# Conditioning in blocks of 1024 columns, four K tiles per visit and two wide groups in a hybrid retention and mLSTM step

## The chip, the cores and the metric

The kernel runs on one core of one Trainium2 chip. The metric is the device time of a run in microseconds. Before the change the median of three runs is 2097.72 us (2091.96 to 2099.7).

The core has several engines with their own instruction queues: TensorE (PE in the profile; PEld is its weight load), VectorE (DVE), ScalarE (ACT), GpSimd (POOL) and SyncE (SP), from whose queue most loads are issued. Some DMAs are issued from GpSimd's queue, in order with its arithmetic.

## The reference

One layer is computed for 128 context tokens (the prompt) and 256 latent tokens (the sample), of width 2048. A conditioning vector for each of the two kinds of tokens is multiplied with `w_mod` to six parts of 2048 numbers: shift, scale and gate of the mixer (parts 0, 1, 2) and of the channel mixer (parts 3, 4, 5).

```
mod_ctx = silu(c_ctx) @ w_mod + b_mod          # w_mod is 2048 x 12288
mod_lat = silu(c) @ w_mod + b_mod
sh1, sc1, g1, sh2, sc2, g2 = split(mod, 6)
h = ln(x) * (1 + sc1) + sh1
mix = mixer(h)                                 # h @ w_in, 8 heads, then @ w_out
x = ln(ALPHA * x + g1 * mix) * ln1_g + ln1_b
h = ln(x) * (1 + sc2) + sh2
x = ln(ALPHA * x + g2 * ffn(h)) * ln2_g + ln2_b
```

The mixer has four retention heads and four mLSTM heads of 256 columns, run forwards and backwards; `ffn` is a gated convolution with 5504 inner columns. All is fp32. The outputs are both kinds of tokens and the final states of the prompt.

## The kernel before

There are 384 tokens, three tiles of 128 (`NT`), and 2048 features, 16 K tiles of 128 (`KT`). Weights and activations are split into a rounded high part and a rest (`split`, L116: a ScalarE cast gives `hi`, a subtraction gives `lo`), and each product is three matmuls: high by high, high by rest, rest by high (`mm_a`, L179, and `mm_b`, L186). The rest of a weight block is made on VectorE, and every so-manieth on GpSimd: every sixth in stage one and in the mixer, none in the output projection, every second in the first part of the channel mixer (`share_splits`, L127).

The program is written against tiles and buffers; a planner works out the waits and the order of each engine's queue, from the order of the program and from its own estimates of the times. A buffer of a pool with `bufs=1` is written again only when its last reader is done, and a DMA that waits for that holds up what stands behind it in its queue.

**Conditioning.** It is computed in two ways, piece by piece between other work. A `Stepper` (L297) holds a generator and, at each step of the main work, lets it go on by so many pieces (its rate).

- `mod_tensor` (L246) computes by features on TensorE: for each K tile one product with the two conditioning vectors, padded to 32 columns (`ct`), into one of four column groups of a PSUM bank (`g = kt % 4`, 32 partitions each), so that the groups hold partial sums. ScalarE copies the bank (`mr`), small products add up the groups and turn the row into columns (`modf`), and VectorE adds the bias. One visit takes `nk` K tiles. It serves parts 0 and 1 in stage one and half of part 4 in the output projection.
- `mod_vector` (L270) computes by rows on VectorE: blocks of 512 columns, for each K tile and each of the two vectors one multiply-add over 512 columns (L287, L284 for the first) into `acc` (`macc`). At the end of a block two products with ones, into column groups 0 and 1, sum over the partitions (L292), VectorE adds the bias (L293), and two stores from GpSimd's queue write the rows into DRAM (`modrow`, L295). The block's bias `bt` is loaded from GpSimd's queue (L276); `acc` and `bt` have one buffer each. It serves parts 2 and 3 and the other half of part 4 (`NV = 2` blocks) in the mixer and part 5 in the channel mixer. `vec_raws` loads two K tiles by 512 columns at a time (512 KB, L234), from SP's queue, where the weights (L141) are loaded too.

**Stage one** (L373 to L471) normalises the tokens and then goes through the K tiles in groups (`groups`): for each group `hs` modulates and splits its K tiles, and `units` multiplies them with the weights of two retention heads; the partial sums go from PSUM into SBUF, added by VectorE from the second group on (`spill`, L388). While a group is multiplied, the conditioning of the next one runs in the `Stepper` at 1.2 pieces per unit, of which there are six a group. The groups are 1, 1, 2, 2, 2, 2, 2, 2 and 2 K tiles, nine in all; a visit's load is always 1 MB, so it has 16, or 8, K tiles of one or two columns' tiles.

**Mixer** (L473 to L866). First come constants and gates (`log_sigmoid`, L508), rotary embedding and the attention of the first two heads; then six more heads, each projected (`proj_a`, `proj_b`) while the attention of the one two places earlier runs. After each weight block comes a step of `mods2` (L614) at rate 0.9. `gnr` and `gnm` (L482 to L485) are rows of the heads' norms, loaded at the beginning and read by `head_tail` (L663 or L665).

**Output projection** (L911 to L959): four blocks of 512 columns by 16 K tiles, two K tiles to a weight block. In the second and third block a step of `mods4` (L927), rate 1.5, follows each weight block; it visits two K tiles of 512 columns at a time (`nk = 2`), with five buffers of 512 KB loaded four ahead. `mod_from_rows` fetches the rows of parts 3 and 4 that the mixer stored.

**Channel mixer** (L1051 on): the up projections with `mods5` (L1120, part 5, rate 0.85) in the first twelve tiles, then the down projections and the last norm.

Of the kernel before, what the change touches and what calls it, by code (L numbers as in the profile page):

```python
# [9 lines left out]
F32 = mybir.dt.float32  # L10
# [5 lines left out]
P = 128  # L16
D = 2048
# [65 lines left out]
def hybrid_step(ctx, tc, ca, cb, x_prompt, x_sample, state_ret, state_c, state_n, state_m, c, c_ctx,  # L83
# [143 lines left out]
    def mod_loads(newraw, pieces, lag):  # L227
        """The pieces' loads in turn, each lag pieces ahead of its use."""
# [11 lines left out]
    NV = 2  # L240

    def vec_raws(mp, blocks):
        return mod_loads(lambda: mp.tile([P, 1024], F32, tag="mraw", name="mraw"),
                         [(q, 2, part * D + j * 512, 512) for part, j in blocks for q in range(0, KT, 2)], 2)

    def mod_tensor(part, k0, n, psp, sbp, raws, nk):  # L246
        """Blocks of the conditioning by features: products on the tensor engine."""
# [22 lines left out]
    def mod_vector(part, psp, mp, raws, js=range(4)):  # L270
        """A part of the conditioning by rows: products on the vector engine, into DRAM."""
        for j in js:
            col = part * D + j * 512
            acc = mp.tile([P, 2, 512], F32, tag="macc", name="macc", bufs=1)
            bt = mp.tile([64, 512], F32, tag="mbt", name="mbt", bufs=1)
            nc.gpsimd.dma_start(out=bt, in_=b_mod[:, col:col + 512].to_broadcast([64, 512]))  # L276
            for q in range(8):
                raw = next(raws)
                for kk in range(2):
                    kt = 2 * q + kk  # L280
                    for v in range(2):
                        src = raw[:, kk * 512:(kk + 1) * 512]
                        if kt == 0:
                            nc.vector.tensor_scalar(out=acc[:, v, :], in0=src, scalar1=ct[:, kt, v:v + 1],  # L284
                                                    scalar2=None, op0=ALU.mult)
                        else:
                            nc.vector.scalar_tensor_tensor(out=acc[:, v, :], in0=src, scalar=ct[:, kt, v:v + 1],  # L287
                                                           in1=acc[:, v, :], op0=ALU.mult, op1=ALU.add)
                yield
            ps = psp.tile([64, 512], F32, tag="ps", name="modr")  # L290
            for v in range(2):
                nc.tensor.matmul(ps[32 * v:32 * v + 32, :], lhsT=ones, rhs=acc[:, v, :], start=True, stop=True)  # L292
            nc.vector.tensor_tensor(bt, ps, bt, op=ALU.add)  # L293
            for v in range(2):
                nc.gpsimd.dma_start(out=modrow[part, v:v + 1, j * 512:(j + 1) * 512], in_=bt[32 * v:32 * v + 1, :])  # L295
# [77 lines left out]
    groups = [(0, 1), (1, 1)] + [(k, 2) for k in range(2, KT, 2)]  # L373
# [39 lines left out]
    with ExitStack() as p0:  # L413
# [51 lines left out]
        for g in range(len(groups)):  # L465
            nxt = Stepper(mods(g + 1) if g + 1 < len(groups) else iter(()), 1.2)
# [7 lines left out]
    with p1:  # L474
# [4 lines left out]
        with tc.issue_after(on_pool[0]):  # L479
            cs = tab.tile([P, C_B], F32, name="cs")  # L480
            nc.gpsimd.dma_start(out=cs, in_=cb)
            gnr = tab.tile([P, 1024], F32, name="gnr")  # L482
            rows_bcast(gnr, gn_ret.rearrange("a h v -> a (h v)"), 1024)
            gnm = tab.tile([P, 1024], F32, name="gnm")
            rows_bcast(gnm, gn_mlstm.rearrange("a h v -> a (h v)"), 1024)  # L485
# [22 lines left out]
        def log_sigmoid(dst, x, shape, tg):  # L508
            def tmp(n):
                return gp.tile(shape, F32, tag=f"ls{tg}{n}", name=f"ls{tg}{n}")  # L510
            e, u, dd, ln = tmp(0), tmp(1), tmp(2), tmp(3)
# [3 lines left out]
            nc.vector.tensor_scalar(out=dd, in0=u, scalar1=-1.0, scalar2=None, op0=ALU.add)  # L515
            nc.vector.tensor_tensor(dd, e, dd, op=ALU.subtract)
            nc.scalar.activation(ln, u, AF.Ln)
            nc.vector.reciprocal(u, u)
            nc.vector.tensor_tensor(dd, dd, u, op=ALU.mult)
            nc.vector.tensor_tensor(ln, ln, dd, op=ALU.add)  # L520
            nc.vector.scalar_tensor_tensor(out=dst, in0=x, scalar=0.0, in1=ln, op0=ALU.min, op1=ALU.subtract)

        log_sigmoid(lgb, lgb, [P, 8], "t")
# [21 lines left out]
        # gates  # L545
# [67 lines left out]
        raws2 = vec_raws(mp, [(part, j) for part in (2, 3) for j in range(4)] + [(4, j) for j in range(NV)])  # L613
# [81 lines left out]
        def mlstm_attn(h, q, k, vx, og):  # L695
# [65 lines left out]
            finish = head_tail(hh, og, gnm, h, 8 + 2 * h, h == NH - 1)  # L761
# [86 lines left out]
        deferred = []  # L848
        for pf, af, h in heads:
            fn, ph, got = pend.pop(0)  # L850
            deferred.append(fn(ph, *got))
            pend.append((af, h, pf(h)))
        mods2.finish()
# [57 lines left out]
    with ExitStack() as p2:  # L911
# [5 lines left out]
        for kt in range(KT - 2, KT):  # L917
# [18 lines left out]
        def w_out_block(nb, ks):  # L936
            ps = [(pat if nb == 1 else pmm).tile([P, 512], F32, tag="ps", name="pso") for _ in range(NT)]
            for k0 in range(0, ks, 2):
# [12 lines left out]
                if nb == 2 and k0 == 8:  # L951
                    mod_from_rows(4, 4 * NV, pat, sb2, "sc2", 1.0)
# [252 lines left out]
```

## Time and profile before

| what | value |
|---|---|
| median of three runs | 2097.72 us |
| range of the runs | 2091.96 to 2099.7 us |
| profiled execution, first to last instruction (its span) | 2095.7 us |
| mean granted TensorE clock | 0.983 |
| DMA traffic | 352.34 MB, mean 168 GB/s |
| `raw<-in_w_in` loads of 256 KB / 512 KB | 152 / 48 |
| `mraw<-in_w_mod` loads of 512 KB | 128 |
| `wm<-in_w_mod` loads of 1 MB | 32 |

For the profiled execution no other time is given than its span; it lies within the range of the timed runs. The profile's page gives busy times of the engines, the span in 40 slices, the chain of work that ended last, and the costliest groups of instructions by line, with their count, busy time, mean duration and what ended the idle time ahead of them. The other views used here are busy time by stretches of the span (its columns are the stretch, its length, then busy time and count for PE, PEld, DVE, ACT and POOL, the granted clock, the DMA share and GB/s), the timeline of one engine (start, duration, engine, line, operation, output and inputs, count, and in square brackets the idle time before it and what ended it), the waits summed by who waited for whom (total, times, longest), and the instructions of one tile (least, median and greatest duration in ns, first and last start). The stages lie in the span as follows: stage one up to about 230 us, the mixer to about 820, the output projection to about 910, the norms after it to about 990, the channel mixer to the end.

### The profile page before, as it was taken

What the parts mean: (1) busy time and instruction counts of PE and PEld (TensorE: products, weight loads), DVE (VectorE), ACT (ScalarE), POOL (GpSimd) and SP (SyncE); (2) the same over time, 40 slices, a digit from 0 to 9 for tenths busy, and PEclk for the clock granted to TensorE, in tenths of its full rate; (3) what the DMA queues carried; (4) which work ended last, traced back from release to release, by engine and by line L of the source; (5) the groups of instructions that cost most, each with busy time, mean ns of one, the idle gap of its engine ahead of it and who ended that gap; (6) DMA issues with size and microseconds to landing.
All of it is one profiled execution on the core that took longest, in us unless ns stands there. A gap on an engine that the chain in (4) does not pass through costs nothing.

```text
span 2095.7 us, 27032 instructions
## 1 busy us (share of the span) xinstructions
PE 2016.2 (96%) x10361; PEld 1758.6 (84%) x10361; DVE 1308.6 (62%) x2095; ACT 683.3 (33%) x1053; POOL 316.6 (15%) x246
## 2 busy tenths in 40 slices
PE   6999899999999998998999999999999999999996
PEld 4777678798888876676998988999989998999985
DVE  4666879888798765367787744444344444444458
ACT  4223333233344443126322322333222332233331
POOL 1111333232122211014234300000000000000004
PEclk9999999999999999998999999999999999999998
DMA  9975777777796535733656644444334443434441
GB/s 330 349 238 189 115 169 214 211 206 232 194 210 191 153 120 189 276 117 102 194 183 202 220 137 130 122 121 130 121 129 123 122 130 121 129 113 131 145 148 70
DMA packets 283296, 352.34 MB, mean 168 GB/s; under 512 B 16271, under 2 KB 213200, under 8 KB 282016
## 3 DMA queue, kind: packets, MB, share of 16 engines
q1 hardware_dynamic: 278896, 340.09, 54.2%
q0 software_dynamic: 4272, 10.54, 1.5%
q8 instruction: 81, 1.33, 0.3%
q14 instruction: 47, 0.39, 0.1%
HBM read 343.16 MB, written 7.41 MB: 167 GB/s over the span
## 4 chain that ended last, share of the span: by engine, by line
PE 81%; DVE 8%; DMA 4%; issue 2%; POOL 2%; SPq 1%; ACT 1%; POOLq 0%; DVEq 0%; ACTq 0%
PE psu L184 11%; PE psu L182 11%; PE psu L183 11%; PE psd L192 5%; PE psd L190 5%; PE psd L191 5%; PE psb L190 3%; PE psb L191 3%; PE psa L182 3%; PE psb L192 3%; DVE macc L287 3%; PE psa L184 3%; PE psa L183 3%; PE modps L255 2%; PE pso L190 2%
## 5 line engine op out<-in xcount | busy, mean ns | idle before, releaser
L118 DVE TENSOR_TENSOR lo<-raw,hi 128x1024 fp32r<-128x1024 f32 (+3 forms) x437 | 454.4, 1048 | 504.3 <-ACT hi L117 504.0
L117 ACT CAST hi<-raw 128x1024 fp32r<-128x1024 f32 (+3 forms) x487 | 436.5, 908 | 952.6 <-PE psu L183 350.8
L184 PE MATMUL psu<-ah,lo 128*128 128x384 f32 x1376 | 467.3, 340 | 9.4 <-DVE lo L118 4.8
L183 PE MATMUL psu<-al,hi 128*128 128x384 f32 x1376 | 467.7, 340 | 0.0
L182 PE MATMUL psu<-ah,hi 128*128 128x384 f32 x1376 | 467.1, 341 | 0.0
L287 DVE SCALAR_TENSOR_TENSOR macc<-mraw,ct,macc 128x512 f32<-128x512 f32 x420 | 348.9, 878 | 28.7 <-DMA mraw<-in_w_mod 28.7
L184 PEld LDWEIGHTS psu<-ah,lo 128*128 128x128 f32 x1376 | 259.5, 189 | 10.0 <-DVE lo L118 5.1
L182 PEld LDWEIGHTS psu<-ah,hi 128*128 128x128 f32 x1376 | 259.5, 189 | 3.5 <-ACT y L1084 0.8
L183 PEld LDWEIGHTS psu<-al,hi 128*128 128x128 f32 x1376 | 259.5, 189 | 0.1
L118 POOL TENSOR_TENSOR lo<-raw,hi 128x1024 fp32r<-128x1024 f32 (+1 forms) x50 | 154.4, 3091 | 392.5 <-ACT hi L117 358.5
L192 PE MATMUL psd<-hi,fal 128*128 128x512 f32 (+1 forms) x484 | 191.3, 395 | 0.0
L191 PE MATMUL psd<-lo,fah 128*128 128x512 f32 (+1 forms) x484 | 189.5, 392 | 0.0
L190 PE MATMUL psd<-hi,fah 128*128 128x512 f32 (+1 forms) x484 | 188.1, 393 | 0.0
L182 PE MATMUL psa<-ah,hi 128*128 128x384 f32 x512 | 180.1, 355 | 1.7 <-DVE og L392 1.7
L184 PE MATMUL psa<-ah,lo 128*128 128x384 f32 x512 | 176.5, 347 | 5.1 <-POOL lo L118 3.6
L183 PE MATMUL psa<-al,hi 128*128 128x384 f32 x512 | 178.1, 348 | 0.0
L200 POOL TENSOR_TENSOR brs<-veps,mhalf 128x1 f32<-128x1 f32 x12 | 13.4, 1116 | 994.0 <-DVE veps L198 993.9
L191 PE MATMUL psb<-lo,ah 128*128 128x512 f32 x384 | 154.1, 401 | 3.3 <-POOL lo L118 2.5
L192 PE MATMUL psb<-hi,al 128*128 128x512 f32 x384 | 153.2, 399 | 0.0
L190 PE MATMUL psb<-hi,ah 128*128 128x512 f32 x384 | 151.2, 405 | 0.3 <-ACT hi L117 0.3
L182 PEld LDWEIGHTS psa<-ah,hi 128*128 128x128 f32 x512 | 98.0, 192 | 19.0 <-issue 11.3
L191 PEld LDWEIGHTS psd<-lo,fah 128*128 128x128 f32 x484 | 90.8, 188 | 22.5
(300 smaller groups left out, 2408.9 us busy)
## 6 DMA issues: line engine op xcount, KB each, us to landing
raw<-in_w_up SPq DMA_DIRECT2D x168, 512.0 KB, 3.7
mraw<-in_w_mod SPq DMA_DIRECT2D x128, 512.0 KB, 5.4
raw<-in_w_down SPq DMA_DIRECT2D x84, 512.0 KB, 3.6
raw<-in_w_in SPq DMA_DIRECT2D x152, 256.0 KB, 5.1
wm<-in_w_mod SPq DMA_DIRECT2D x32, 1024.0 KB, 7.9
raw<-in_w_in SPq DMA_DIRECT2D x48, 512.0 KB, 6.9
raw<-in_w_out SPq DMA_DIRECT2D x32, 512.0 KB, 4.2
out<-r SPq DMA_DIRECT2D x12, 256.0 KB, 2.0
```

Source lines behind the costliest of these rows:

```text
L117: nc.scalar.copy(dst_hi, src)
L118: mark["lo"] = (eng or nc.vector).tensor_tensor(out=dst_lo, in0=src, in1=dst_hi.bitcast(F32), op=ALU.subtract).ins
L182: nc.tensor.matmul(ps, lhsT=hi[:, s], rhs=ah, start=start, stop=False)
L183: nc.tensor.matmul(ps, lhsT=hi[:, s], rhs=al, start=False, stop=False)
L184: nc.tensor.matmul(ps, lhsT=lo[:, s], rhs=ah, start=False, stop=stop)
L190: nc.tensor.matmul(ps, lhsT=ah[:, t], rhs=hi[:, s], start=start, stop=False)
L191: nc.tensor.matmul(ps, lhsT=ah[:, t], rhs=lo[:, s], start=False, stop=False)
L192: nc.tensor.matmul(ps, lhsT=al[:, t], rhs=hi[:, s], start=False, stop=stop)
L200: mark["pow"] = nc.gpsimd.tensor_tensor(out=out, in0=v[:, :n], in1=mhalf[:, :n], op=ALU.pow).ins
L255: nc.tensor.matmul(ps[32 * g:32 * g + 32, :w], lhsT=ct[:, kt, :], rhs=raw[:, kk * w:(kk + 1) * w], start=kt < 4, stop=kt >= 12)
L287: nc.vector.scalar_tensor_tensor(out=acc[:, v, :], in0=src, scalar=ct[:, kt, v:v + 1], in1=acc[:, v, :], op0=ALU.mult, op1=ALU.add)
```

## The change

- `mod_vector` works in blocks of 1024 columns: `acc` is 128 x 2 x 1024, a load is one K tile by 1024 columns, a multiply-add covers 1024 columns, and the block's sums are four products into all four column groups, followed by one addition over 128 partitions and four stores; the bias comes in two loads. `NV` is 1 block, which is the same half of part 4.
- `mods4` takes four K tiles per visit: loads of 1 MB in three buffers, two ahead, at rate 0.9.
- The last eight K tiles of stage one form two groups of four in place of four groups of two; ahead of a group of four the conditioning runs at 2.0 pieces per unit. Its visits then have four K tiles of 512 columns, and the weight blocks of `q` and `k` four K tiles.
- `gnm` shares one buffer with `gnr` and is loaded once the first mLSTM head is at the front of the pending heads. `log_sigmoid` works with two temporaries fewer and one VectorE instruction fewer.

```diff
-    NV = 2
+    NV = 1
...
-                         [(q, 2, part * D + j * 512, 512) for part, j in blocks for q in range(0, KT, 2)], 2)
+                         [(kt, 1, part * D + j * 1024, 1024) for part, j in blocks for kt in range(KT)], 2)
...
+    def mod_vector(part, psp, mp, raws, js=range(2)):
...
+            col = part * D + j * 1024
+            acc = mp.tile([P, 2, 1024], F32, tag="macc", name="macc", bufs=1)
+            bt = mp.tile([P, 512], F32, tag="mbt", name="mbt", bufs=1)
+            for hf in range(2):
+                nc.gpsimd.dma_start(out=bt[64 * hf:64 * hf + 64, :],
+                                    in_=b_mod[:, col + hf * 512:col + (hf + 1) * 512].to_broadcast([64, 512]))
+            for kt in range(KT):
                 raw = next(raws)
+                for v in range(2):
+                    if kt == 0:
+                        nc.vector.tensor_scalar(out=acc[:, v, :], in0=raw, scalar1=ct[:, kt, v:v + 1],
+                                                scalar2=None, op0=ALU.mult)
+                    else:
+                        nc.vector.scalar_tensor_tensor(out=acc[:, v, :], in0=raw, scalar=ct[:, kt, v:v + 1],
+                                                       in1=acc[:, v, :], op0=ALU.mult, op1=ALU.add)
                 yield
+            ps = psp.tile([P, 512], F32, tag="ps", name="modr")
+            for hf in range(2):
+                for v in range(2):
+                    g = 2 * hf + v
+                    nc.tensor.matmul(ps[32 * g:32 * g + 32, :], lhsT=ones, rhs=acc[:, v, hf * 512:(hf + 1) * 512],
+                                     start=True, stop=True)
             nc.vector.tensor_tensor(bt, ps, bt, op=ALU.add)
+            for hf in range(2):
+                for v in range(2):
+                    g = 2 * hf + v
+                    nc.gpsimd.dma_start(out=modrow[part, v:v + 1, j * 1024 + hf * 512:j * 1024 + (hf + 1) * 512],
+                                        in_=bt[32 * g:32 * g + 1, :])
...
-    groups = [(0, 1), (1, 1)] + [(k, 2) for k in range(2, KT, 2)]
+    groups = [(0, 1), (1, 1), (2, 2), (4, 2), (6, 2), (8, 4), (12, 4)]
...
-            nxt = Stepper(mods(g + 1) if g + 1 < len(groups) else iter(()), 1.2)
+            wide = g + 1 < len(groups) and groups[g + 1][1] == 4
+            nxt = Stepper(mods(g + 1) if g + 1 < len(groups) else iter(()), 2.0 if wide else 1.2)
...
-            nc.vector.tensor_scalar(out=dd, in0=u, scalar1=-1.0, scalar2=None, op0=ALU.add)
-            nc.vector.tensor_tensor(dd, e, dd, op=ALU.subtract)
+            nc.vector.scalar_tensor_tensor(out=e, in0=u, scalar=-1.0, in1=e, op0=ALU.add, op1=ALU.subtract)
...
+            if pend[0][0] is mlstm_attn and not gn_m:
+                gn_m.append(tab.tile([P, 1024], F32, tag="gn", name="gnm"))
+                rows_bcast(gn_m[0], gn_mlstm.rearrange("a h v -> a (h v)"), 1024)
...
-        mp = pool("mp2", 5, p2m, reuse_waits="tile")
-        raws4 = mod_loads(lambda: mp.tile([P, 1024], F32, tag="mraw", name="mraw"),
-                          [(q, 2, 4 * D + j * 512, 512) for j in range(NV, 4) for q in range(0, KT, 2)], 4)
-        mods4 = Stepper(chain(*[mod_tensor(4, 4 * j, 4, pmm, sb2, raws4, 2) for j in range(NV, 4)]), 1.5)
+        mp = pool("mp2", 3, p2m, reuse_waits="tile")
+        raws4 = mod_loads(lambda: mp.tile([P, 2048], F32, tag="mraw", name="mraw"),
+                          [(q, 4, 4 * D + j * 512, 512) for j in range(2 * NV, 4) for q in range(0, KT, 4)], 2)
+        mods4 = Stepper(chain(*[mod_tensor(4, 4 * j, 4, pmm, sb2, raws4, 4) for j in range(2 * NV, 4)]), 0.9)
```

More of the change, by code (lines that the diff above doesn't have):

```diff
@@ L268, in mod_tensor @@
         yield
-    def mod_vector(part, psp, mp, raws, js=range(4)):
+    def mod_vector(part, psp, mp, raws, js=range(2)):
         for j in js:
[L273 to L277, printed above, removed]
-                raw = next(raws)
[L279 to L288, printed above, removed]
-                yield
[L290 to L295, printed above, removed]
@@ L481, in hybrid_step @@
             nc.gpsimd.dma_start(out=cs, in_=cb)
-            gnr = tab.tile([P, 1024], F32, name="gnr")
+            gnr = tab.tile([P, 1024], F32, tag="gn", name="gnr")
             rows_bcast(gnr, gn_ret.rearrange("a h v -> a (h v)"), 1024)
-            gnm = tab.tile([P, 1024], F32, name="gnm")
-            rows_bcast(gnm, gn_mlstm.rearrange("a h v -> a (h v)"), 1024)
             m0b = tab.tile([P, 8], F32, name="m0b")
@@ L510, in tmp @@
                 return gp.tile(shape, F32, tag=f"ls{tg}{n}", name=f"ls{tg}{n}")
-            e, u, dd, ln = tmp(0), tmp(1), tmp(2), tmp(3)
+            e, u, ln = tmp(0), tmp(1), dst
             nc.scalar.activation(e, x, AF.Abs)
@@ L514, in log_sigmoid @@
             nc.vector.tensor_scalar(out=u, in0=e, scalar1=1.0, scalar2=None, op0=ALU.add)
-            nc.vector.tensor_scalar(out=dd, in0=u, scalar1=-1.0, scalar2=None, op0=ALU.add)
-            nc.vector.tensor_tensor(dd, e, dd, op=ALU.subtract)
+            nc.vector.scalar_tensor_tensor(out=e, in0=u, scalar=-1.0, in1=e, op0=ALU.add, op1=ALU.subtract)
             nc.scalar.activation(ln, u, AF.Ln)
             nc.vector.reciprocal(u, u)
-            nc.vector.tensor_tensor(dd, dd, u, op=ALU.mult)
-            nc.vector.tensor_tensor(ln, ln, dd, op=ALU.add)
+            nc.vector.tensor_tensor(e, e, u, op=ALU.mult)
+            nc.vector.tensor_tensor(ln, ln, e, op=ALU.subtract)
             nc.vector.scalar_tensor_tensor(out=dst, in0=x, scalar=0.0, in1=ln, op0=ALU.min, op1=ALU.subtract)
-        log_sigmoid(lgb, lgb, [P, 8], "t")
+        lth = lgb
+        lgb = tab.tile([P, 8], F32, name="lgb2")
+        log_sigmoid(lgb, lth, [P, 8], "t")
         def rope(dst, a, b, sb):
@@ L610, in hybrid_step @@
         sb = pool("sb1", 2, p1, reuse_waits="tile")
-        raws2 = vec_raws(mp, [(part, j) for part in (2, 3) for j in range(4)] + [(4, j) for j in range(NV)])
+        raws2 = vec_raws(mp, [(part, j) for part in (2, 3) for j in range(2)] + [(4, j) for j in range(NV)])
         mods2 = Stepper(chain(mod_vector(2, pat, mp, raws2), mod_vector(3, pat, mp, raws2),
@@ L760, in mlstm_attn @@
                                                        in1=hh[:, tt, :], op0=ALU.mult, op1=ALU.add)
-            finish = head_tail(hh, og, gnm, h, 8 + 2 * h, h == NH - 1)
+            finish = head_tail(hh, og, gn_m[0], h, 8 + 2 * h, h == NH - 1)
             for d in range(2):
@@ L847, in hybrid_step @@
         pend = [(ret_attn, h, first[h]) for h in range(2)]
-        deferred = []
+        deferred, gn_m = [], []
         for pf, af, h in heads:
@@ L951, in w_out_block @@
                 if nb == 2 and k0 == 8:
-                    mod_from_rows(4, 4 * NV, pat, sb2, "sc2", 1.0)
+                    mod_from_rows(4, 8 * NV, pat, sb2, "sc2", 1.0)
             return ps
@@ L1119, in hybrid_step @@
     mp3 = pool("mp3", 3, p3m, reuse_waits="tile")
-    mods5 = Stepper(mod_vector(5, pps, mp3, vec_raws(mp3, [(5, j) for j in range(4)])), 0.85)
+    mods5 = Stepper(mod_vector(5, pps, mp3, vec_raws(mp3, [(5, j) for j in range(2)])), 0.85)
     a += ups(2, 10)
```

## Prediction

> **What bounds the kernel now.** I read the page first, then busy time by stage, because its shares are averages over stages with different limits.
>
> ```profile
> span 2095.7 us, 27032 instructions
> PE 2016.2 (96%) x10361; PEld 1758.6 (84%) x10361; DVE 1308.6 (62%) x2095; ACT 683.3 (33%) x1053; POOL 316.6 (15%) x246
> ```
>
> ```profile
> 0.00:220.00 220.00, 200.27 (x1345) 150.49 (x1346) 139.66 (x338) 71.52 (x169) 28.16 (x29) 1.00 0.83 268
> 300.00:820.00 520.00, 506.07 (x2401) 429.82 (x2400) 418.21 (x719) 196.65 (x337) 133.36 (x114) 0.99 0.65 184
> 820.00:910.00 90.00, 90.00 (x376) 59.30 (x376) 36.85 (x44) 22.78 (x23) 1.12 (x2) 0.98 0.81 281
> 1200.00:2050.00 850.00, 850.00 (x4367) 786.57 (x4366) 381.74 (x493) 259.08 (x305) 0.00 (x0) 1.00 0.42 129
> ```
>
> The columns are the stretch, its length, busy time of PE, PEld, DVE, ACT and POOL, granted clock, DMA share and GB/s. TensorE is the bound: full in the output projection (820 to 910), 506 of 520 us in the mixer, full in the untouched last 850 us. VectorE, at 418 of 520 us in the mixer, has slack there. So a microsecond taken from TensorE's own instructions comes straight off the end; one taken from VectorE counts only where TensorE waits for it. I therefore sum two things: PE work removed, and PE waits removed.
>
> **PE work: visits and sums.** The conditioning products run with 32 output columns, four column groups to a bank. I read their form groups and four stretches of PE's timeline.
>
> ```profile
> L292 PE MATMUL modr<-macc,ones 128*32 128x512 f32 x56 | 16.4, 605 | 0.0
> L255 PE MATMUL modps<-mraw,ct 128*32 128x512 f32 x64 | 15.8, 605 | 0.0
> ```
>
> ```profile
> 830.05 0.39 PE L192 MATMUL pso<-hi,al 128*128 128x512 f32 x1
> 830.37 1.05 PE L255 MATMUL modps<-mraw,ct 128*32 128x512 f32 x4
> ...
> 831.70 0.39 PE L191 MATMUL pso<-lo,ah 128*128 128x512 f32 x1
> ...
> 834.36 1.06 PE L255 MATMUL modps<-mraw,ct 128*32 128x512 f32 x8
> ```
>
> ```profile
> 308.95 1.01 PE modr L292 x4
> ```
>
> In the output projection each visit is two K tiles, so two of the four groups; fp32 shows as two instructions a product, hence x4, and 64 instructions are 16 visits. A visit takes 1.05 us. At 834.36 two neighbouring visits happen to stand side by side, with eight instructions in all four groups, and take 1.06 us together: the other two groups are free. That is what the change makes of every visit.
>
> What a visit costs PE: from 830.05 to 831.70 are 1.65 us, in which two ordinary 512-column products also start. Without a visit between, such a product takes about 0.238 us (an estimate: the full 90 us of the stage, less its visits' 15.8, over its 376 - 64 = 312 other instructions). So a visit costs 1.65 - 0.48 = 1.17 us. Fifteen stand apart now (16, one pair merged), eight after: 7 x 1.17 = 8.2 us.
>
> The sums of `mod_vector` have the same shape: four instructions in two groups, 1.0 us on the chain, 56 / 4 = 14 of them. After: seven sums of eight instructions in four groups, at the price of the 834.36 row: again 7 x 1.17 = 8.2 us. Together **-16.4 us**; the other bound is nothing, if eight instructions did not overlap as in that row (rival 2).
>
> **VectorE.** 420 multiply-adds over 512 columns become 210 over 1024.
>
> ```profile
> L287 DVE SCALAR_TENSOR_TENSOR macc<-mraw,ct,macc 128x512 f32<-128x512 f32 x420 | 348.9, 878 | 28.7 <-DMA mraw<-in_w_mod 28.7
> L118 DVE TENSOR_TENSOR lo<-raw,hi 128x1024 fp32r<-128x1024 f32 x325 | 398.7, 1227 | 468.8 <-ACT hi L117 468.7
> L118 DVE TENSOR_TENSOR lo<-raw,hi 128x512 fp32r<-128x512 f32 x40 | 27.0, 685 | 24.8 <-ACT hi L117 24.6
> ```
>
> The split instruction shows what another 512 columns cost: 1227 - 685 = 542 ns. So a wide multiply-add is about 878 + 542 = 1420 ns, and 210 of them 298 us: 51 us less VectorE, nearly all in stretches where it has slack. Taken at nothing by itself; it counts below, where PE waits.
>
> **Block ends.** After a block's sum GpSimd stores two rows, and its next bias load must wait until they have landed, as `bt` has one buffer. What is queued behind that load on GpSimd is every sixth (later every second) weight split, which PE needs.
>
> ```profile
> POOL mbt L276 <- DMA modrow<-mbt: 28.2, 7, 7.2
> ```
>
> ```profile
> 356.57 1.09 POOL L295 DMA_DIRECT2D modrow<-mbt  x2 [2.55 <-DVE mbt L293]
> 362.72 0.55 POOL L276 DMA_DIRECT2D mbt<-in_b_mod  x1 [5.07 <-DMA modrow<-mbt]
> 363.28 9.52 POOL L118 TENSOR_TENSOR lo<-raw,hi 128x512 fp32r<-128x512 f32 x2
> ```
>
> ```profile
> 1105.00 11.56 POOL L118 TENSOR_TENSOR lo<-raw,hi 128x1024 fp32r<-128x1024 f32 x2
> ```
>
> ```profile
> 370.65 0.44 PE L184 MATMUL psa<-ah,lo 128*128 128x384 f32 x1 [1.31 <-POOL lo L118]
> 372.85 0.69 PE L184 MATMUL psa<-ah,lo 128*128 128x384 f32 x1 [1.41 <-POOL lo L118]
> ```
>
> ```profile
> 713.35 0.53 PE L191 MATMUL psb<-lo,ah 128*128 128x512 f32 x1 [2.53 <-POOL lo L118]
> ```
>
> ```profile
> 1114.29 0.69 PE L184 MATMUL psu<-ah,lo 128*128 128x384 f32 x1 [4.54 <-POOL lo L118]
> ```
>
> ```profile
> 366.00:380.00 14.00, 11.28 (x55) 10.63 (x55) 11.07 (x13) 2.10 (x2) 9.08 (x4) 0.88 0.39 120
> 708.00:722.00 14.00, 11.47 (x46) 9.34 (x45) 4.95 (x8) 4.49 (x7) 5.81 (x2) 0.88 0.42 131
> 1108.00:1122.00 14.00, 9.46 (x39) 9.13 (x39) 6.24 (x11) 2.22 (x3) 8.55 (x2) 0.76 0.49 166
> ```
>
> Three of the 14 ends stop PE: for 2.72, 2.53 and 4.54 us, 9.8 in all. The granted clock falls right after (0.88, 0.88 and 0.76 over 14 us): lost 14 x 0.12 = 1.7, 1.7 and 14 x 0.24 = 3.4 us, 6.8 in all. Together 16.6 us, 1.2 us per end. [...]
>
> Seven ends are left. At the same price each, 8.3 us go. But each now queues four stores and two bias loads on GpSimd where it queued two and one, and the splits behind still compete with multiply-adds; at double price nothing goes. What waits is mostly the landing (28.2 / 7 = 4.0 us), which doesn't double, so I take **-5 us**, bounds -8 and +3.
>
> **The end of stage one.** Nine groups become seven, so two rounds of 20 partial-sum additions go from VectorE.
>
> ```profile
> L392 DVE TENSOR_TENSOR vx<-psb,vx 128x256 f32<-128x256 f32 x48 | 20.2, 421 | 23.9 <-PE psb L192 23.8
> L392 DVE TENSOR_TENSOR q<-psa,q 128x384 f32<-128x384 f32 x32 | 17.2, 553 | 13.0 <-PE psa L184 12.8
> ```
>
> ```profile
> 215.00:240.00 25.00, 17.99 (x79) 11.19 (x77) 25.00 (x47) 8.66 (x16) 10.54 (x7) 0.92 0.57 86
> 240.00:260.00 20.00, 19.50 (x94) 18.98 (x94) 15.97 (x27) 6.38 (x10) 7.93 (x4) 0.85 1.03 158
> ```
>
> ```profile
> 219.36 0.41 PE L182 MATMUL psa<-ah,hi 128*128 128x384 f32 x1 [1.69 <-DVE og L392]
> ```
>
> ```profile
> 240.48 0.69 PE L184 MATMUL psa<-ah,lo 128*128 128x384 f32 x1 [1.52 <-DVE lo L118]
> ```
>
> A round is 12 narrow and 8 wide additions (the `og` and `k` rows are alike): 12 x 0.42 + 8 x 0.55 = 9.5 us. One of the two rounds goes from the last 30 us, where VectorE is full (25.00 of 25) and PE waits for it 1.69 and 1.52 us. I take **-3 us** for those two; bounds 0 and -8, the latter if the clock (0.92 and 0.85: 25 x 0.08 + 20 x 0.15 = 5.0 us) also stays up.
>
> PE's own work in stage one doesn't change: a wide visit is eight 512-column instructions, 1.06 us, a present one sixteen of 256.
>
> ```profile
> 75.62 1.93 PE L255 MATMUL modps<-wm,ct 128*32 128x256 f32 x32
> ```
>
> That row is two present visits, 0.97 us each; four visits a part for four tiles before and after.
>
> **What is put in the way.** Stage one's wide group must have 8.4 MB of `w_mod` (two parts, 2048 x 512 words) before its first product, 4.2 more than now. In the output projection three loads of 1 MB stand ahead of the weights in SP's queue at the start of the second block where five of 0.5 did: 0.5 MB at 281 GB/s is 1.9 us. I charge **+2 us**, bounds 0 and +6.
>
> ```profile
> 60.00:120.00 60.00, 59.53 (x422) 44.59 (x414) 39.72 (x97) 17.11 (x38) 6.08 (x3) 1.00 1.02 333
> ```
>
> At 60 to 120 us DMA is full (1.02, 333 GB/s), yet PE idles only 0.47 us: transfers run well ahead.
>
> **At nothing:** the later `gn_mlstm` load, since its buffer is free after the last of the first row and needed at the first of the second, 80 us later, with only GpSimd's own work queued behind:
>
> ```profile
> L665 POOL TENSOR_TENSOR og<-og,gnr x4: 1802/1912/2257, 222.3 to 418.8; 128x768 f32<-128x768 f32 x4
> ```
>
> ```profile
> L665 POOL TENSOR_TENSOR og<-og,gnm x3: 1816/1841/1947, 499.1 to 662.9; 128x768 f32<-128x768 f32 x3
> ```
>
> Without that cover it would hold up one normalisation of a head, whose transposes are deferred anyway. The shorter `log_sigmoid` is one short VectorE instruction less per call, under other products. The stepping rates keep pace: six units at 2.0 make the 12 steps of a wide group, 16 blocks at 0.9 make 14 for the 12 of the output projection.
>
> **The sum.** -16.4 - 5 - 3 + 2 = -22.4 us on the profiled span of 2095.7, which has 2.0 us less than the median of the runs (2097.72); nothing else is shown around it. Predicted median: 2097.7 - 22.4 = 2075 us. A measurement here can tell about 0.5%, 10.5 us, from no change.
>
> **Rivals.**
>
> 1. *Stage one waits for its wide group.* If the 4.2 MB came on top at 333 GB/s, the first wide group would start 12.6 us late, and the clock would drop once (1.7): 2075 + 14 = 2089, no change to tell. For: DMA is full until 120 us. Against: PE's 0.47 us of idleness. Chance 0.16.
> 2. *Four groups don't overlap*, and the change doesn't do what it says: eight visits then cost as much as fifteen, and so do the sums: 2075 + 16.4 = 2091. Against it stands the row of 834.36. Chance 0.05.
> 3. *Slower, by the block ends.* A wide multiply-add holds VectorE for about 1.4 us where a narrow one held it 0.9; the split that started at 1105.00 took with its neighbour 11.56 us among them. Should each of the seven ends now cost what the worst costs today, 4.54 + 3.4 = 7.9 us, they cost 55 instead of 16.6: 2075 + 5 + 39 = 2119. The other terms give -17.4, so it decides, slower by 10.5, from (10.5 + 17.4 + 16.6) / 7 = 6.4 us an end, against 1.2 today. [...] Chance 0.06.
> 4. *More than forecast*: every end and the whole of 215 to 260 us come free, -16.4 - 16.6 - 8 = -41: 2057. Chance 0.07.
>
> **The numbers.** Forecast 0.66, its own range 2062 to 2087. The range 2060 to 2094 takes in rivals 1 and 2 and leaves out 3, 4 and the tails, under 0.2. Faster: 0.66 + 0.07 and a quarter of rival 1, 0.77. Slower: 0.06. The rest, 0.17, is the same.
>
> **What would show it.** Right: `modps` on `mraw` as eight instructions per visit in about 1.05 us, eight visits; seven `modr` sums of eight; fewer PE waits on GpSimd's `lo` between 300 and 1200 us; fewer PE waits around 215 to 245 us; PE without gaps at 90 to 140 us. Wrong: a PE gap of several us ahead of K tile 8; visits of 2 us; GpSimd splits over 9 us at most of the block ends.

## The result and the profile after

The changed kernel takes 2083.19 us (median of four runs, 2081.45 to 2084.25), the kernel before, run beside it, 2098.31: a ratio of 0.9938, 95% interval 0.9922 to 0.9955, or 15.1 us less. The forecast was 2075, 22.4 less. The profiled execution took 2084.25 us, with a span of 2082.5.

The page of the changed kernel, its first lines:

```profile
span 2082.5 us, 26370 instructions
PE 1993.8 (96%) x10233; PEld 1753.3 (84%) x10233; DVE 1260.7 (61%) x1803; ACT 683.8 (33%) x1035; POOL 287.2 (14%) x245
```

TensorE still bounds: its busy time fell by 22.4 us, the span by 13.2. So 9.2 us of what PE gained came back as waiting. The same stretches as in the prediction show where (stretch, length, PE, PEld, DVE, ACT, POOL, clock, DMA share, GB/s):

```profile
0.00:220.00 220.00, 191.22 (x1177) 141.99 (x1178) 139.09 (x287) 67.22 (x147) 24.66 (x28) 0.96 0.88 283
300.00:820.00 520.00, 508.73 (x2450) 438.82 (x2449) 381.17 (x563) 199.19 (x343) 118.84 (x116) 0.99 0.65 181
820.00:910.00 90.00, 90.00 (x414) 64.79 (x413) 43.87 (x53) 23.96 (x24) 1.12 (x2) 1.00 0.81 287
1200.00:2050.00 850.00, 850.00 (x4367) 786.62 (x4366) 391.02 (x513) 257.58 (x304) 2.31 (x3) 1.00 0.41 125
```

Stage one is worse: PE is busy 191.22 us of the first 220, where it was 200.27, and the granted clock is 0.96 in place of 1.00. To place gains and losses I compare, in both traces, when PE has started the same amount of its main products (those of the projections, the output projection among them, and of the channel mixer, which the change leaves alone). After against before that is +10.9 us at 207 us of the kernel before, +7.8 at 329, +1.3 at 437, -1.7 at 785, -9.9 at 912, behind the output projection, and -13.3 from 1154 to the end. The gain is made in the mixer, the output projection and the channel mixer; stage one gives some 11 us away.

**The sums and visits are what was forecast.** PE's groups, and two places of its timeline:

```profile
L255 PE MATMUL modps<-mraw,ct 128*32 128x512 f32 x64 | 9.4, 603 | 0.0
L293 PE MATMUL modr<-macc,ones 128*32 128x512 f32 x56 | 7.5, 604 | 0.0
```

```profile
361.39 1.06 PE L293 MATMUL modr<-macc,ones 128*32 128x512 f32 x8
...
830.50 1.06 PE L255 MATMUL modps<-mraw,ct 128*32 128x512 f32 x8
```

Eight instructions in four groups take 1.06 us, as the row at 834.36 had it. PE is busy 15.3 us less on the two groups together (16.4 + 15.8 against 7.5 + 9.4).

**The block ends are quieter.** The bias load waits behind the stores 4 times for 15.9 us (7 times, 28.2 before), and no split on GpSimd takes over 4.4 us, where the longest before took 10.8 (tile view of each, least, median and greatest ns). First after, then before:

```profile
POOL mbt L277 <- DMA modrow<-mbt: 15.9, 4, 4.8
```

```profile
L118 POOL TENSOR_TENSOR lo<-raw,hi x49: 1277/2406/4384, 42.3 to 1164.9; 128x1024 fp32r<-128x1024 f32 x39, 128x512 fp32r<-128x512 f32 x10
```

```profile
L118 POOL TENSOR_TENSOR lo<-raw,hi x50: 1267/2405/10785, 40.2 to 1178.2; 128x1024 fp32r<-128x1024 f32 x42, 128x512 fp32r<-128x512 f32 x8
```

**A new wait stands in stage one.** It is ahead of the second wide group, K tiles 12 to 15. PE's timeline of the changed kernel, then ScalarE's row between, then VectorE's:

```profile
172.51 1.92 PE L255 MATMUL modps<-wm,ct 128*32 128x512 f32 x16
...
182.91 0.95 PE L264 MATMUL modf<-cst,mr 128*128 128x2 f32 x8
194.19 1.65 PE L182 MATMUL psa<-ah,hi 128*128 128x384 f32 x4 [10.33 <-DVE h L337]
```

```profile
174.51 0.59 ACT L259 COPY mr<-modps 128x512 f32<-128x512 f32 x1 [0.88 <-PE modps L255]
```

```profile
182.55 2.48 DVE L286 SCALAR_TENSOR_TENSOR macc<-mraw,ct,macc 128x1024 f32<-128x1024 f32 x2 [1.71 <-DMA mraw<-in_w_mod]
184.95 0.42 DVE L397 TENSOR_TENSOR vx<-psb,vx 128x256 f32<-128x256 f32 x1
...
186.27 1.28 DVE L286 SCALAR_TENSOR_TENSOR macc<-mraw,ct,macc 128x1024 f32<-128x1024 f32 x1
...
188.13 1.28 DVE L286 SCALAR_TENSOR_TENSOR macc<-mraw,ct,macc 128x1024 f32<-128x1024 f32 x1
189.32 0.16 DVE L267 TENSOR_TENSOR sc<-modf,bmc 128x8 f32<-128x8 f32 x1
...
190.53 2.48 DVE L286 SCALAR_TENSOR_TENSOR macc<-mraw,ct,macc 128x1024 f32<-128x1024 f32 x2
192.93 1.25 DVE L337 TENSOR_SCALAR h<-xnt,sc,sh 128x128 f32<-128x128 f32 x4
```

The conditioning's products end at 174.5 us, but the `modf` products behind them stand in PE's queue after the rest of the present group and start at 182.91. Then `sc` and `h` stand in VectorE's queue behind multiply-adds of the *mixer's* conditioning, whose first sum runs at 361 us. PE waits 10.33 us. The granted clock is down in that place, 0.78 over 30 us:

```profile
170.00:200.00 30.00, 19.27 (x90) 15.12 (x89) 22.51 (x33) 4.94 (x8) 1.56 (x2) 0.78 0.64 212
```

The question for the experiments: did this wait cost the missing 7 us, and are the other parts worth what the prediction gave them?

### The profile page after: what moved, and what is told of

Read it like the earlier page. It is cut to its first block, busy times and chain, and to the rows that moved or that the text cites. A ratio compares the mean times of both kernels' runs of the same rounds, so it can differ in the third digit from the quotient of the medians.

```text
span 2082.5 us, 26370 instructions
## 1 busy us (share of the span) xinstructions
PE 1993.8 (96%) x10233; PEld 1753.3 (84%) x10233; DVE 1260.7 (61%) x1803; ACT 683.8 (33%) x1035; POOL 287.2 (14%) x245
## 4 chain that ended last, share of the span: by engine, by line
PE 80%; DVE 10%; DMA 4%; issue 3%; SPq 1%; ACT 1%; POOL 0%; POOLq 0%; DVEq 0%; ACTq 0%
PE psu L184 10%; PE psu L182 10%; PE psu L183 10%; PE psd L192 5%; PE psd L190 5%; PE psd L191 5%; DVE macc L286 4%; PE psb L190 4%; PE psb L191 4%; PE psb L192 3%; PE psa L182 3%; PE psa L184 3%; PE psa L183 3%; PE pso L190 2%; DMA raw<-in_w_in 2%
## 5 line engine op out<-in xcount | busy, mean ns | idle before, releaser
L286 DVE SCALAR_TENSOR_TENSOR macc<-mraw,ct,macc 128x1024 f32<-128x1024 f32 x210 | 311.7, 1521 | 14.1 <-DMA mraw<-in_w_mod 14.0
L182 PE MATMUL psa<-ah,hi 128*128 128x384 f32 x512 | 180.8, 357 | 14.1 <-DVE h L337 10.3
L118 POOL TENSOR_TENSOR lo<-raw,hi 128x1024 fp32r<-128x1024 f32 (+1 forms) x49 | 124.3, 2540 | 398.8 <-ACT hi L117 342.2
```

Source lines behind the costliest of these rows:

```text
L118: mark["lo"] = (eng or nc.vector).tensor_tensor(out=dst_lo, in0=src, in1=dst_hi.bitcast(F32), op=ALU.subtract).ins
L182: nc.tensor.matmul(ps, lhsT=hi[:, s], rhs=ah, start=start, stop=False)
L286: nc.vector.scalar_tensor_tensor(out=acc[:, v, :], in0=raw, scalar=ct[:, kt, v:v + 1], in1=acc[:, v, :], op0=ALU.mult, op1=ALU.add)
```

## The experiments

Every kernel was timed in five rounds beside the kernel before on its own chip. The differences are of medians, on that chip.

| kernel | us | against before | ratio, 95% interval |
|---|---|---|---|
| changed, narrow stage one | 2098.31 | +3.1 | 1.0013 (1.0003 to 1.0022) |
| changed, only the first wide group | 2087.89 | -7.3 | 0.9974 (0.9963 to 0.9985) |
| changed, multiply-adds behind stage one | 2082.97 | -12.2 | 0.9946 (0.9933 to 0.9958) |
| before + wide groups | 2091.93 | -3.3 | 0.9988 (0.9979 to 0.9996) |
| before + visits | 2087.94 | -7.6 | 0.9962 (0.9950 to 0.9974) |
| before + blocks | 2105.14 | +9.7 | 1.0045 (1.0031 to 1.0058) |
| before + blocks, sums by halves | 2104.27 | +8.8 | 1.0037 (1.0025 to 1.0050) |
| before, bias load later | 2096.05 | +0.6 | 1.0003 (0.9994 to 1.0013) |
| before + wide groups + visits | 2086.36 | -8.5 | 0.9956 (0.9943 to 0.9968) |
| before + blocks, behind the gates | 2074.92 | -20.0 | 0.9900 (0.9886 to 0.9914) |
| changed, behind the gates | 2066.66 | -28.2 | 0.9860 (0.9845 to 0.9875) |
| before, behind the gates | 2095.31 | +0.9 | 1.0002 (0.9993 to 1.0011) |

### Is the new wait the loss?

**The changed kernel with the old nine groups.**

```diff
-    groups = [(0, 1), (1, 1), (2, 2), (4, 2), (6, 2), (8, 4), (12, 4)]
+    groups = [(0, 1), (1, 1)] + [(k, 2) for k in range(2, KT, 2)]
```

> The changed kernel with the nine groups of stage one as they were before. Theory: of the changed kernel's time, 10.3 us of PE idleness at 184 to 194 us and some 3 us of half clock behind it come from the second wide group, whose modulation stands on VectorE behind multiply-adds of the mixer's conditioning; with narrow groups it should go, less the two rounds of partial-sum additions that come back: 2083 - 8 = about 2075 us. Rival (the wait is only moved: VectorE has the same work and PE will wait for it elsewhere before the mixer): 2081 to 2085 us.

Measured 2098.31 us: without the wide groups, which bring the wait, the kernel loses all of its gain. The theory that the wait is a plain loss fell, and the rival was too small as well. The wait of 10.3 us is gone, but others have come, between stage one and the mixer (PE's waits of 160 to 330 us: total, times, longest):

```profile
PE psa L182 <- DVE k L397: 5.5, 1, 5.5
PE num L836 <- DVE at L805: 5.0, 1, 5.0
PE psa L184 <- POOL lo L118: 3.4, 1, 3.4
PE psa L184 <- DVE lo L118: 2.6, 1, 2.6
```

**Only the first wide group.**

```diff
+    groups = [(0, 1), (1, 1), (2, 2), (4, 2), (6, 2), (8, 4), (12, 2), (14, 2)]
```

> The changed kernel with one wide group only, K tiles 8 to 11; tiles 12 to 15 in two groups of two. Theory: the long wait belongs to a wide group at the end of stage one, when the planner has already begun the next stage's multiply-adds; with narrow groups at the end no PE wait over 4 us is left ahead of 230 us, about 2075 us. Rival (any wide group waits, because four tiles are modulated in a row): a wait of 5 us or more ahead of K tile 8 or 12, 2080 us or more.

Measured 2087.89 us, between the two: each wide group earns something, the second too, in spite of its wait. Neither the theory nor the rival foresaw the wait that is left: PE waits 7.5 us for `h` at 206 us, ahead of K tiles 14 and 15, a narrow group. So it does not take a group of four at the end to make it.

**The multiply-adds behind stage one.** The steps of the mixer's conditioning are issued only after the last split of stage one's activations.

```diff
+                mark["hs"] = mark["lo"]
...
+        def step2():
+            with tc.issue_after(mark["hs"]):
+                mods2.step()
...
-                mods2.step()
+                step2()
```

> The changed kernel; the mixer's conditioning on VectorE is put behind the last split of stage one's last group, nothing else. Theory (order on VectorE makes the wait): the bias addition and the modulation follow the sums by 3 to 4 us and not by 9, the wait falls from 10.3 to about 5 us, and with the clock the time to about 2076 us. Rival (the wait comes from the late small products on PE, at 182.9 us, 8 us after their input was ready): the wait stays over 8 us and the time at 2081 to 2085 us.

Measured 2082.97 us, as the changed kernel: the wait fell further than the theory asked, and the time did not follow. In place the edit does what it should: PE waits 1.51 us for `h` in place of 10.33, and at 207 us this kernel is 2.8 us ahead of the kernel before, where the changed one was 10.9 behind. But the multiply-adds now stand a little later in the same queue, ahead of the gates. PE's row, then VectorE's:

```profile
234.24 0.69 PE L182 MATMUL psa<-ah,hi 128*128 128x384 f32 x1 [5.16 <-DVE gi L577]
```

```profile
225.76 4.02 DVE L286 SCALAR_TENSOR_TENSOR macc<-mraw,ct,macc 128x1024 f32<-128x1024 f32 x2
...
230.38 3.41 DVE L286 SCALAR_TENSOR_TENSOR macc<-mraw,ct,macc 128x1024 f32<-128x1024 f32 x2
233.70 0.54 DVE L577 COPY gi<-gsel 4x384 f32<-4x384 f32 x1
```

The wait has moved, not gone. What matters, it seems, is the whole passage from stage one into the mixer, about 180 to 330 us.

### What is each part worth alone?

**The wide groups alone, on the kernel before.**

```diff
+    groups = [(0, 1), (1, 1), (2, 2), (4, 2), (6, 2), (8, 4), (12, 4)]
...
+            wide = g + 1 < len(groups) and groups[g + 1][1] == 4
+            nxt = Stepper(mods(g + 1) if g + 1 < len(groups) else iter(()), 2.0 if wide else 1.2)
```

> The kernel before with nothing but the two wide groups and their rate of 2.0. Theory: the wide groups alone cost what they cost in the changed kernel, 5 to 11 us, the multiply-adds over 512 columns being in the way as well: 2103 to 2109 us, with a PE wait of 5 us or more ahead of K tile 12. Rival (the wait needs the wider multiply-adds): no change, 2095 to 2100 us.

Measured -3.3 us (interval of the ratio below 1): neither the loss of the theory nor the rival's same time. Narrow multiply-adds make PE wait as well, 6.95 us ahead of the second wide group:

```profile
186.43 1.65 PE L182 MATMUL psa<-ah,hi 128*128 128x384 f32 x4 [6.95 <-DVE h L332]
```

So much of the new wait comes with the wide groups themselves; with the wider blocks it is 3.4 us longer. The passage behind it then runs better than before: from 1.1 us behind at 207 us to 7.4 ahead at 308.

**The four-tile visits alone.**

```diff
-        mp = pool("mp2", 5, p2m, reuse_waits="tile")
+        mp = pool("mp2", 3, p2m, reuse_waits="tile")
...
+                          [(q, 4, 4 * D + j * 512, 512) for j in range(NV, 4) for q in range(0, KT, 4)], 2)
+        mods4 = Stepper(chain(*[mod_tensor(4, 4 * j, 4, pmm, sb2, raws4, 4) for j in range(NV, 4)]), 0.9)
```

> The kernel before with nothing but the four-tile visits in the output projection. Forecast's term: 7 visits less at 1.17 us, -8.2 us: 2090 us. Rival (the output projection waits for its larger loads instead): 2095 us or more, with PE waits on DMA between 820 and 910 us.

Measured -7.6 us: the term of 8.2 is right, and PE is busy on the visits 9.6 us in place of 15.8.

**The wider blocks alone** (narrow stage one, two-tile visits; the change of `gnm` and `log_sigmoid` is in).

```diff
-    groups = [(0, 1), (1, 1), (2, 2), (4, 2), (6, 2), (8, 4), (12, 4)]
+    groups = [(0, 1), (1, 1)] + [(k, 2) for k in range(2, KT, 2)]
...
-                          [(q, 4, 4 * D + j * 512, 512) for j in range(2 * NV, 4) for q in range(0, KT, 4)], 2)
+                          [(q, 2, 4 * D + j * 512, 512) for j in range(2 * NV, 4) for q in range(0, KT, 2)], 4)
```

> The kernel before with nothing but the blocks of 1024 columns, their sums in four groups, and the shared buffer and shorter helper that make room for them. Forecast's terms: seven sums less at 1.17 us (-8.2) and fewer block ends (-5, bounds -8 and +3): 2085 us. Rival (the ends cost more each, since four stores and two loads queue on GpSimd): 2090 us or more.

Measured 2105.14 us: *slower* by 9.7, though the sums' group on PE is down to 7.5 us as in the changed kernel. Against the kernel before this one is 9.7 us behind at 248 us, 21.6 at 308, and wins only part of it back, 7.9 at the end. The passage, in VectorE's waits of 180 to 330 us, VectorE's timeline and PE's:

```profile
DVE macc L286 <- DMA mraw<-in_w_mod: 8.6, 2, 4.9
```

```profile
220.47 2.40 DVE L286 SCALAR_TENSOR_TENSOR macc<-mraw,ct,macc 128x1024 f32<-128x1024 f32 x1 [4.88 <-DMA mraw<-in_w_mod]
222.80 0.41 DVE L118 TENSOR_TENSOR lo<-raw,hi 128x256 fp32r<-128x256 f32 x1
223.13 0.54 DVE L397 TENSOR_TENSOR k<-psa,k 128x384 f32<-128x384 f32 x1
```

```profile
223.82 0.66 PE L182 MATMUL psa<-ah,hi 128*128 128x384 f32 x1 [5.53 <-DVE k L397]
```

VectorE is not busy here: it stands still for 4.88 us, because the multiply-add at the head of its queue waits for its load, and the split and the partial sum behind it, which PE waits for, could have run: ScalarE's casts for the one had ended at 215.3 us, PE's products for the other at 214.7. The kernel before loses 2.1 us in two such waits in this passage, this one 8.6.

The size of a block adds to it. In both kernels one block of the mixer's conditioning stands in the passage, 32 multiply-adds, and the next one starts only behind its sum (at 309 us before, at 375 here). The 32 narrow ones keep VectorE busy for 24.8 us, the 32 wide ones for 40.7. The rival, dearer block ends, is not what happened: no bias load waits for the stores in this trace, and the longest split on GpSimd takes 4.5 us.

**The sums one half after the other**, in two column groups each, to show what the four groups bring.

```diff
+            for hf in range(2):
+                ps = psp.tile([P, 512], F32, tag="ps", name="modr")[64 * hf:64 * hf + 64, :]
...
+                    nc.tensor.matmul(ps[32 * v:32 * v + 32, :], lhsT=ones, rhs=acc[:, v, hf * 512:(hf + 1) * 512],
+                                     start=True, stop=True)
```

> As the run with the blocks alone, but a block's sums are made in two steps, each in two column groups of a bank of its own, with an addition each. Theory: two sums in two groups cost twice the PE time of one in four, so 7 x 1.17 = 8 us more than the blocks alone; the gain of the ends stays. Rival (what the blocks bring comes from their fewer ends and wider multiply-adds, not from the packing): within 3 us of the blocks alone.

Measured 2104.27 us, no different, but the run decides nothing: the halves were placed side by side in groups 0, 1 and 2, 3 and still overlapped in five of the seven sums (9.5 us of PE in all).

**The bias load later, on the kernel before**, to price its wait on the stores.

```diff
             for q in range(8):
                 raw = next(raws)
+                if q == 4:
+                    nc.gpsimd.dma_start(out=bt, in_=b_mod[:, col:col + 512].to_broadcast([64, 512]))
```

> The kernel before; a block's bias is loaded after four of its eight pieces and not at its start, nothing else. Theory: GpSimd's queue no longer waits at the block ends for the stores to land, so the weight splits behind it come in time: of the 16.6 us that the ends cost, 8 or more go, 2088 to 2091 us, and the waits of GpSimd on the stores (28.2 us) go. Rival (the splits are late because VectorE's multiply-adds hold GpSimd off, not because of the landing): 2095 to 2100 us, with splits of over 9 us still there.

Measured no difference, and again nothing decided: the planner still put the load early in GpSimd's queue, where it waited seven times, 25.5 us (28.2 before).

**Wide groups and visits without the blocks** (both edits above).

> The kernel before with the two wide groups of stage one and the four-tile visits of the output projection, and its own conditioning blocks of 512 columns. Theory: the wider blocks bring nothing of their own, because alone they cost 9.7 us at the transition from stage one to the mixer while their sums save 8 us of PE; without them the two other parts add up: 2095.5 - 3.3 - 7.6 = about 2084 to 2085 us, the time of the changed kernel within 3 us. Rival: once the wide groups are in, the blocks give their 8 us of PE back in full; then this kernel lies 8 us above the changed one, at 2091 us or more.

Measured 2086.36 us, -8.5. The rival of 2091 or more fell. By the ratios the blocks add 0.9956 - 0.9938 = 0.0018, 3.8 us, and the intervals overlap: in the changed kernel the wider blocks bring little or nothing.

### Where the blocks' gain went

The parts do not add up: visits, wide groups and blocks alone make -7.6 - 3.3 + 9.7 = -1.2 us, all three together -15.1. If the blocks lose at the passage, it must help to keep their multiply-adds out of it.

**The blocks alone, behind the gates.** Steps of the mixer's conditioning are issued only after the copy of the gates' columns, the last of the gates' work.

```diff
-        nc.vector.tensor_copy(gcol, pc2)
+        mark["gate"] = nc.vector.tensor_copy(gcol, pc2).ins
...
+        def step2():
+            with tc.issue_after(mark["gate"]):
+                mods2.step()
...
-                mods2.step()
+                step2()
```

> The kernel with the wider blocks alone (2105 us), in which the steps of the mixer's conditioning are issued only behind the copy of the gates' columns, so that no multiply-add of the mixer's conditioning stands in VectorE's queue during the transition. Theory: the 9.7 us that the blocks cost come from these multiply-adds of some 1.3 us each, put ahead of the split additions and partial sums of the transition; behind the gates the loss goes, and the 8 us that the sums save on PE show: 2087 to 2092 us. Half of it (2095 to 2099) if the multiply-adds then meet the mixer's own work later. Rival: the loss is not the multiply-adds' place but something else that the wider blocks bring (their bias loads, their bigger buffers): 2103 to 2107 us, as without the delay.

Measured 2074.92 us: 30 us less than the same kernel without the delay, more than the theory asked for. The engines in the passage and in the 70 us behind it; first the passage of the kernel before, then the blocks without the delay, then with it:

```profile
200.00:330.00 130.00, 119.53 (x557) 97.67 (x556) 108.04 (x198) 47.13 (x84) 42.33 (x37) 0.95 0.73 156
```

```profile
200.00:330.00 130.00, 105.48 (x469) 87.91 (x469) 107.72 (x168) 41.28 (x73) 53.67 (x32) 0.84 0.69 160
330.00:400.00 70.00, 70.00 (x363) 63.04 (x362) 42.53 (x57) 26.54 (x50) 20.14 (x21) 1.00 0.60 162
```

```profile
200.00:330.00 130.00, 123.78 (x623) 105.31 (x622) 114.17 (x180) 55.16 (x98) 42.99 (x35) 0.99 0.84 182
330.00:400.00 70.00, 70.00 (x347) 61.35 (x346) 66.70 (x74) 22.15 (x37) 18.98 (x21) 1.00 0.79 238
```

In the same 130 us PE runs 623 instructions in place of 469, at a clock of 0.99 in place of 0.84. Waiting and clock share the loss: PE is busy 18.3 us less without the delay, and the lower clock over its 105.48 busy us is worth another 16 us or so, an estimate (105.48 x 0.15). VectorE does *more* in the passage with the delay, 114.17 us: it was not overfull, its queue was in the wrong order. Its row of the mixer's multiply-adds from 160 to 330 us, without the delay and with it, says the same:

```profile
L286 DVE SCALAR_TENSOR_TENSOR macc<-mraw,ct,macc x30: 1177/1267/2401, 209.4 to 298.1; 128x1024 f32<-128x1024 f32 x30
```

```profile
L286 DVE SCALAR_TENSOR_TENSOR macc<-mraw,ct,macc x30: 1250/1274/2320, 265.0 to 329.5; 128x1024 f32<-128x1024 f32 x30
```

With the two that open the block there are 32 both times, only later: the first starts at 263.2 us in place of 207.2.

**The changed kernel, behind the gates** (the same edit).

> The changed kernel with the same delay: the mixer's conditioning behind the copy of the gates' columns. Theory: the wait of 10.3 us in front of h in stage one goes, and so do the waits of the transition to which they moved when the steps stood behind the last split of stage one: 2074 to 2079 us. Rival: VectorE is full there with splits and additions in any case, and multiply-adds that are held back only meet the mixer later: 2082 to 2086 us, no difference.

Measured 2066.66 us, the fastest of all, 0.9860 of the kernel before and, by the two ratios, 0.8% or some 16 us under the changed kernel. The rival fell, and the theory was too modest. It lies 8.3 us below the blocks alone behind the gates. If the visits are worth there the 7.6 that they brought alone, the wide groups bring next to nothing with the passage clear; no run shows that by itself.

**The kernel before, behind the gates** (the same edit).

> The kernel before, unchanged but for the same delay: the steps of its mixer's conditioning, blocks of 512 columns, are issued only behind the copy of the gates' columns. With the delay the wider blocks alone gave 2074.9 us. Theory: the wider blocks are worth what the prediction put down for them, some 13 us (8 of PE and 5 at the blocks' ends), as soon as their multiply-adds are kept out of the transition; then this kernel takes about 2088 us, and the delay itself brings some 7 us with the narrow blocks. Rival: the delay brings the whole 20 us whatever the width, and the blocks are worth nothing: 2075 to 2078 us. In between (2080 to 2085) the sums' 8 us of PE show and the blocks' ends bring nothing.

Measured 2095.31 us, no change; neither the theory nor the rival foresaw that. The delay works in the passage here too: at 308 us this kernel is 12.9 us ahead of the kernel before, the blocks behind the gates 12.3. But by 386 us it has only 4.7 left, where the other has 17.2. The stretch behind the passage, a split on GpSimd in it, and PE's row behind that:

```profile
200.00:330.00 130.00, 125.74 (x612) 105.58 (x611) 113.09 (x199) 55.12 (x95) 38.66 (x37) 0.97 0.80 165
330.00:400.00 70.00, 62.80 (x291) 53.05 (x290) 59.43 (x96) 18.35 (x35) 30.50 (x20) 0.95 0.68 208
```

```profile
L118 POOL TENSOR_TENSOR lo<-raw,hi x50: 1260/2402/10957, 40.0 to 1174.2; 128x1024 fp32r<-128x1024 f32 x42, 128x512 fp32r<-128x512 f32 x8
```

```profile
367.47 0.69 PE L184 MATMUL psa<-ah,lo 128*128 128x384 f32 x1 [4.65 <-POOL lo L118]
```

```profile
L292 PE MATMUL modr<-macc,ones 128*32 128x512 f32 x56 | 19.5, 604 | 0.9 <-DVE hmv L660 0.9
```

With narrow blocks PE is busy 62.80 of the 70 us, with wide ones all of them. A GpSimd split takes 10.96 us and PE waits 4.65 us for it, and four of the sums (one, before) run in two separate halves, so that the sums keep PE busy for 19.5 us. Out of the passage, then, the wider blocks are worth about 20 us (2095.31 against 2074.92, by the ratios 1.0%), more than the 13 that the prediction gave to sums and block ends.

## Why the prediction was right or wrong

The forecast of 22.4 us stands against 15.1, inside the range and with the sign foretold, but it came out so by errors that cancel. That the time fell into the range is in good part luck.

- **PE work, -16.4: right.** The visits measured -7.6 alone, against -8.2. The sums fell as forecast in PE's rows (16.4 us to 7.5); what that is worth in time no run shows by itself. Rival 2, four groups that don't overlap, is out: 1.06 us for eight.
- **VectorE, "taken at nothing by itself": the step that failed.** The wide multiply-add's price was near (1521 ns on average against 1420, 311.7 us in all against 298). But "nearly all in stretches where it has slack" looked at VectorE's busy share and not at its order. The planner issues the mixer's conditioning as early as stage one, and what stood behind one of its multiply-adds in the queue had to wait: in the blocks alone a split and a partial sum behind one that waited 4.88 us for its load, in the changed kernel `sc` and `h` behind those that ran, with a PE wait of 10.33 us. A wide block also puts 15.9 us more of them into the passage (40.7 against 24.8). That made the blocks cost 9.7 us alone and was worth 30 us of difference when they were moved. The stretch of 215 to 240 us with VectorE at 25.00 of 25 stood in the prediction; I read it under the wide groups alone.
- **Block ends, -5: sign right, size not settled.** PE waited 10.6 us for GpSimd splits in the kernel before (the three ends and 0.8 more) and does not wait for any now; its waits for VectorE's splits in the channel mixer are longer, 7.5 us in place of 4.8. The two runs that should have priced the ends apart decided nothing; of the blocks' gain of some 20 us behind the gates, PE's rows have 12.0 on the sums (19.5 against 7.5), and the rest, for ends and slow splits, is not told apart. Rival 3, slower by the ends, named the right sign for the blocks alone but the wrong place: the loss was at the passage, and the ends got better.
- **The end of stage one, -3: met by the wide groups alone (-3.3), but by luck.** That value is net of a wait of 6.95 us that the forecast did not have. In the changed kernel they are worth about 15 us (2098.31 against 2083), apparently because they relieve VectorE in the very passage that the blocks make worse: with them 12 of the 32 multiply-adds run before 200 us and 29.4 us of them are left, without them 40.7. With the passage clear they are worth almost nothing, as far as the difference above tells. A term without its partner was no price for it.
- **"What is put in the way", +2: mis-sized and put on the wrong queue.** I charged the wider groups' loads. DMA held up nothing there: from 60 to 176 us PE waits 0.5 us in all, for ScalarE, and there is no PE gap ahead of K tile 8. The wait came ahead of K tile 12, 10.33 us, with the clock at 0.78 over 30 us, and its cause is the order on PE (`modf` behind the rest of the group) and on VectorE (`h` behind the mixer's multiply-adds). Stage one ends up 11 us late, where rival 1 had 14 by DMA; taken away, that wait came back as others until the multiply-adds were behind the gates.

What stays open: why one load is late in the passage with the wide blocks. SyncE's loads of `w_mod` there wait in turn for VectorE (18.8 us for the multiply-adds, 10.1 for rotary products, from 200 to 330 us of the blocks alone), so the delay may feed itself. Against that, in the kernel before they waited longer for the multiply-adds, 31.9 us, though only 0.3 for rotary products. It was not tried apart.

## What to carry to other kernels

An engine with slack in a stage still had an order here (VectorE stood still 4.88 us behind one late load, and PE waited 5.53 us for what came after it): for each operation that is made longer or moved, ask what stands behind it in its queue and whether its input can be late, above all where a planner fills one stage with the next one's work. Run the parts of a change one by one and in pairs: here one part of three was a loss alone, and without the wide groups the other two together lost 3 us. When a wait is removed and the time stays, look for it further on in the same queue (here 10.33 us became 1.51, and 5.16 us stood ahead of the gates); moving the whole background job behind the crowded passage was worth about as much as the change itself (16 us against 15), though on the kernel before, with its narrow blocks, the same move brought nothing.

## What the hardware showed

**With the wider multiply-adds the longest GpSimd splits were shorter.** In all eight kernels with 1024-column blocks the longest GpSimd split of a weight took 4.1 to 5.8 us, in all six with 512-column blocks 9.6 to 11.0 us. So the splits of over 9 us, which the prediction named as a sign that it was wrong, did not come with the wider ones. The longest split of the kernel before, 10.79 us, ran beside 12 narrow multiply-adds, the longest of the changed kernel, 4.38 us, beside two wide ones. Whether their number or their length decides is not shown: no run changes the one without the other.

**The clock did not follow from the length of one wait.** In the changed kernel it fell after a wait of 2.06 us and stayed up after one of 2.23. PE's rows and the stretches around them:

```profile
251.53 0.45 PE L182 MATMUL psa<-ah,hi 128*128 128x384 f32 x1 [2.06 <-ACT hi L117]
```

```profile
997.10 0.41 PE L182 MATMUL psu<-ah,hi 128*128 128x384 f32 x1 [2.23 <-DVE y L349]
```

```profile
250.00:256.00 6.00, 4.47 (x17) 4.47 (x18) 3.04 (x5) 1.23 (x3) 0.49 (x1) 0.72 1.01 155
996.00:1002.00 6.00, 4.90 (x28) 4.93 (x29) 6.00 (x9) 2.96 (x5) 0.00 (x0) 1.00 0.78 262
```

What else decides it, these runs do not show.
